# Two head pairs of a delta rule in opposite halves of the matrix array, their products by turns

## The chip, the cores and the metric

The kernel runs on one core of one Trainium2 chip. The metric is the device time of one execution in microseconds (us), taken as the median of several runs. One execution more is profiled, and everything below that is told of single instructions comes from its trace.

## The reference, cut to what matters

The program is a trunk of two layers for 256 positions and width 2048: an attention layer, a gated MLP, a layer of RWKV-7 time mixing, and a second gated MLP. The change touches the time mixing alone, 32 heads of width 64 with a matrix state each:

```python
def step(state, inp):
    r_t, w_t, k_t, v_t, kk_t, a_t = inp
    sa = jnp.einsum('bhvk,bhk->bhv', state, -kk_t)
    state = (state * w_t[:, :, None, :] + sa[..., None] * (kk_t * a_t)[:, :, None, :]
             + v_t[..., None] * k_t[:, :, None, :])
    return state, jnp.einsum('bhvk,bhk->bhv', state, r_t)

s0 = jnp.zeros((B, H, N, N), f32)
_, o = lax.scan(step, s0, (tmaj(r4), tmaj(w4), tmaj(k4), tmaj(v4), tmaj(kk), tmaj(a4)))
```

The projections around it are dense products of 2048 by 2048, whose weights are split into a high and a low part.

## The kernel before

**Staging.** The 32 heads are worked off in eight quads of four heads. A quad holds two pairs of heads, z = 0 and z = 1; a pair has 128 channels, so it fills the 128 partitions. The 256 positions are cut into four chunks c of 64, and within a chunk the recurrence is written in closed form: two triangular matrices per head and chunk, the inverse of one of them, and then a walk over the four chunks in which the state `st` is carried.

**What fills TensorE.** The generator `drive` weaves two strands. The filling strand is `quad_in` of the next quad: dense products in units of two K tiles, each unit being four matmuls (lines 154 and 155, or 157 at the end of a sum), with the DVE and ACT work for their weights (`w_hi` on ACT, line 131; `w_lo` on DVE, line 134). The other strand is `quad` of the present quad, a chain in which each step waits for the one before. Where `quad` says `yield n`, n dense units are issued before its next step, so that the evacuation of one step is done while TensorE works on dense units. All yields of a quad add up to 32, the number of units in `quad_in`. The last quad runs over units of the output projection instead, about two for each yield of 1. On TensorE, DVE and ACT the order of instructions is the order of the code; a wait in one of them holds up everything behind it on that engine.

**Steps of `quad` that the change touches**, in order of the code:

- Key norms: `pn` (line 856), then on DVE `kkt` (860), the operands `bk` (861) and `ar` (863); `yield 4`.
- Products of `bk` and `ar` (876) into `AQ`, the transposes of `bk` (888) into `tm`; `yield 4`.
- First level of the inverse by doubling: 901 on TensorE, 903, 905 and 906 on DVE; `yield 1`. Then the levels 2 to 16, each with a product 917, a `yield 1`, a product 928 and a `yield 1`. These work on 32 by 32 tiles, four of them by turns.
- The walk over the chunks c = 0 to 3. In each chunk, with e = c % 2, half e of the 128 partitions holds the chunk's rows of keys, and the other half receives: the state's part (975, not for c = 0), product A (979, contraction over 64 partitions, output in the other 64), an ACT copy to `R` (982), a dense unit, product B (994, `Z` by `R`), a DVE copy to `UV` (996), a dense unit, the state's increment (1003, not for c = 3), product C (1006, contraction over 128, output in 64 partitions), the new state on DVE (1012, 1014), an ACT copy of the chunk's result to `on2` (1021), and one or two dense units.

Each of A, B and C consists of four products, for two pairs z and two heads h. Each stands in the trace as two matmuls, so a step shows as eight. Before the change, all eight of a step use the same half of the partitions for input and the same half for output. The increment (1003) goes the other way: its two heads write to the two halves, and the code issues them by turns. It is the same for the products 876, which read their two heads from the two halves by turns.

The names of banks: `pc` is a part of the twin `pp`, two PSUM banks, one for each pair z. `pU` is one bank `sc` that holds both pairs.

Of the kernel before, what the change touches and what calls it, by code (L numbers as in the profile page):

```python
# [10 lines left out]
F32 = mybir.dt.float32  # L11
F32R = mybir.dt.float32r
AF = mybir.ActivationFunctionType
ALU = mybir.AluOpType
# [3 lines left out]
P = 128  # L18
# [35 lines left out]
class Trunk:  # L54
# [670 lines left out]


    def quad_in(self, j, sp, w, part):

        nc, a, cc, hv = self.nc, self.a, self.cc, self.hv
        tt, act = nc.vector.tensor_tensor, nc.scalar.activation  # L730
        c4 = lambda t: t.rearrange("p (c t) -> p c t", c=4)
# [17 lines left out]
        def receptance(z):  # L749

            ge = lambda t: t.rearrange("p (g e) t -> p g e t", e=2)
            rr = sp.tile([P, S], F32, name="kr", bufs=2)
            rrs.append(rr)
            self.fold(rr, prs[z])
            tt(d["ar"][:, z, :, 0::3], ge(c4(rr)), ge(d["E"][:, z])[:, :, :, 1:65], op=ALU.mult)
            if z == 0:
                nc.vector.scalar_tensor_tensor(rr, rr, self.v("rk", 2 * j), d["kp"][:, 0], op0=ALU.mult, op1=ALU.mult)
# [11 lines left out]
        for z in range(2):  # L769
            p = 2 * j + z  # L770
# [15 lines left out]
            ta = d["ta"][:, z]  # L786
# [7 lines left out]
            E, Ei = d["E"][:, z], d["Ei"][:, z]  # L794
# [3 lines left out]
            kp, g = d["kp"][:, z], flat(cs)[:, 0:S]  # L798
# [35 lines left out]
    def quad(self, j, sp, w):  # L834


        nc, a, cc, vt = self.nc, self.a, self.cc, w["vt"]
        mm, tt = nc.tensor.matmul, nc.vector.tensor_tensor
        Q = range(2)
# [7 lines left out]
        bk = sp.tile([P, 4, 256], F32, name="bk", tag="bkuv")  # L847
        kp4 = d["kp"].rearrange("p z (c e t) -> p (z c) e t", c=2, e=2)
        Ei4 = d["Ei"].rearrange("p z (c e) t -> p (z c) e t", e=2)
        for e in range(2):  # L850
            nc.gpsimd.tensor_mul(bk[:, :, 192 * e:192 * e + 64], kp4[:, :, e], Ei4[:, :, e, 1:65])
        pn = self.bank("sc")
        for z in Q:
# [6 lines left out]
        tt(k2, k2, pn, op=ALU.mult)  # L860
        tt(bk[:, :, 64:192], d["ta"].rearrange("p z (c t) -> p (z c) t", c=2),
           d["kk"].rearrange("p z (c t) -> p (z c) t", c=2), op=ALU.mult)
        tt(d["ar"].rearrange("p z g a t -> p (z g) a t")[:, :, 1:3],
           d["kk"].rearrange("p z (g e t) -> p (z g) e t", g=2, e=2),
           d["E"].rearrange("p z (g e) t -> p (z g) e t", e=2)[:, :, :, 0:64], op=ALU.mult)
        yield 4

# [18 lines left out]
        for z in Q:  # L886
            for c in range(3):
                nc.tensor.transpose(pts[z][:, c * P:(c + 1) * P], bk4[z][:, c], self.ident)
            nc.scalar.copy(flat(tm[:, z]), pts[z][:, 0:384])
# [16 lines left out]
        nc.vector.transpose(flat(Z), flat(X))  # L906
        yield 1

        vq = vt[:, :, 2 * j * P:2 * (j + 1) * P]
        UV = sp.tile([P, 2, 4, P], F32, name="UV", tag="bkuv")  # L910
        for li, b in enumerate(LEVELS):
# [9 lines left out]
            if li < 2:  # L921
                nc.scalar.copy(UV[hs[li], :, li::2], vq[hs[li]].rearrange("p c (z n) -> p z c n", z=2))
            elif li == 2:
                self.sums([d["rk"]], d["bo"][:, 1:2])
# [42 lines left out]
        for c in range(4):  # L967
            g, e = c // 2, c % 2
            hv, hu = hs[e], hs[1 - e]
            uh = lambda z, h: UV[:, z, c, 64 * h:64 * h + 64]  # L970

            pc = po[:, :, c * P:(c + 1) * P]
            if c:
                for z in Q:
                    mm(pc[:, z], ar4[z][:, c], st[:, 2 * z:2 * z + 2].rearrange("p h n -> p (h n)"),
                       start=True, stop=False)
# [13 lines left out]
            yield 1  # L990
            pU = self.bank("sc").rearrange("p (z n) -> p z n", z=2)
            for z in Q:
                for h in range(2):
                    mm(pU[hu, z, h * 64:h * 64 + 64], Z[hu, 4 * z + 2 * h + g], R[hu, z, h * 64:h * 64 + 64],
                       start=True, stop=True)
            nc.vector.tensor_scalar_mul(UV[hu, :, c], pU[hu, :, 0:P], -1.0)
            if c == 3:
                self.moments(d, s6, 0, 1)
            yield 1
            if c < 3:  # L1000
                for z in Q:
                    for h in range(2):
                        mm(pU[hs[h], z, P:P + 64], tm[:, z, c, hs[h]], uh(z, h), start=True, stop=True)
            for z in Q:
                for h in range(2):
                    mm(pc[hv, z, h * 64:h * 64 + 64], AQ[:, 4 * z + 2 * h + g, e, 64 * e:64 * e + 64], uh(z, h),
                       start=c == 0, stop=c == 0 or h == 1)
            if c < 3:
# [10 lines left out]
                else:  # L1019
                    self.moments(d, s6, 0, 0)  # L1020
            nc.scalar.copy(on2[hv, :, g], pc[hv])
            yield (2, 2, 1, 0)[c]
# [241 lines left out]
```

## Time and profile before

| | us |
|---|---|
| median of 3 runs | 2532.43 |
| lowest, highest | 2531.91, 2534.03 |
| the profiled execution, device time | 2531.73 |
| its span from the first to the last instruction | 2529.9 |
| TensorE busy in the span | 2472.4 (98%) |
| VectorE (DVE) busy | 1822.3 (72%) |
| ScalarE (ACT) busy | 1291.8 (51%) |
| GpSimd (POOL) busy | 426.0 (17%) |
| mean granted clock of TensorE | 0.989 of full speed |

The quads stand between about 1250 and 1725 us of the span. A row of a timeline gives the start, the duration, the engine, the line and the tiles; rows of the same kind that follow each other are merged, "x8" being eight of them, and the duration then runs from the first start to the last end. Matmuls overlap, since each takes longer from start to end than the distance to the next.

### The profile page before, as it was taken

How to read it: one execution, taken by the hardware profiler on the slowest of the kernel's cores; microseconds unless marked ns; L12 is line 12 of the kernel's file. 1: busy time of each engine (PE TensorE's matmuls, PEld its weight loads, DVE VectorE, ACT ScalarE, POOL GpSimd, SP SyncE). 2: the span in 40 equal slices, each digit the busy share in tenths (PEclk: the TensorE clock that was granted, in tenths of full speed). 3: DMA queues.
4: the chain of work that ended last, by engine and by line, in shares of the span. 5: the costliest groups of instructions: out<-in, count | busy, mean ns of one | idle time of the engine just before them, and what ended most of it. 6: DMA issues, size and time to landing. Idle time of an engine off the chain costs nothing.

```text
span 2529.9 us, 50155 instructions
## 1 busy us (share of the span) xinstructions
PE 2472.4 (98%) x19492; PEld 2125.1 (84%) x19492; DVE 1822.3 (72%) x3550; ACT 1291.8 (51%) x2706; POOL 426.0 (17%) x650
## 2 busy tenths in 40 slices
PE   8999999999999999989999999999999999999998
PEld 7888888888888888877877777788888888888887
DVE  7768778888888645478676676777888888884544
ACT  6468655555555444454444454445555555554443
POOL 3100112222222100000122222212222222220000
PEclk9999999999999999999999899999999999999999
DMA  7554555655555666646422223235555565556664
GB/s 264 169 181 153 165 181 187 192 190 186 192 189 189 186 189 190 186 140 184 150 91 86 80 92 100 79 119 160 175 190 190 187 191 191 187 186 191 190 187 144
DMA packets 125342, 422.36 MB, mean 167 GB/s; under 512 B 14000, under 2 KB 19504, under 8 KB 125104
## 3 DMA queue, kind: packets, MB, share of 16 engines
q1 hardware_dynamic: 124960, 418.82, 52.3%
q8 instruction: 153, 2.51, 0.4%
q14 instruction: 85, 0.70, 0.1%
q10 hardware_dynamic: 144, 0.33, 0.0%
HBM read 417.00 MB, written 2.10 MB: 166 GB/s over the span
## 4 chain that ended last, share of the span: by engine, by line
PE 90%; DVE 6%; issue 2%; ACT 1%; POOL 0%; DMA 0%; SPq 0%; DVEq 0%; ACTq 0%
PE pd L186 41%; PE pd L187 22%; PE pd L154 6%; PE pd L155 3%; PE pd L189 2%; DVE w_lo L134 1%; PE sc L630 1%; PE pp L231 1%; PE pp L232 1%; PE pp L230 1%; PE pp L928 1%; PE pp L917 1%; PE pd L231 1%; PE pd L230 1%; PE pd L232 1%
## 5 line engine op out<-in xcount | busy, mean ns | idle before, releaser
L116 DVE TENSOR_TENSOR w_lo<-w_raw,w_hi 128x512 fp32r<-128x512 f32 (+1 forms) x1384 | 1052.7, 791 | 314.0 <-ACT w_hi L114 289.0
L186 PE MATMUL pd<-xc,w_hi 128*128 128x512 f32 x3000 | 1057.4, 393 | 2.4 <-DVE u L203 1.1
L114 ACT CAST w_hi<-w_raw 128x512 fp32r<-128x512 f32 (+1 forms) x1384 | 790.7, 617 | 467.2 <-PE pd L186 286.6
L187 PE MATMUL pd<-xc,w_lo 128*128 128x256 f32 x3200 | 868.5, 282 | 1.8 <-DVE w_lo L116 1.8
L186 PEld LDWEIGHTS pd<-xc,w_hi 128*128 128x128 f32 x3000 | 563.5, 188 | 120.0 <-issue 5.2
L187 PEld LDWEIGHTS pd<-xc,w_lo 128*128 128x128 f32 x3200 | 604.4, 189 | 19.1 <-DVE w_lo L116 2.3
L186 PE MATMUL pd<-hc,w_hi 128*128 128x512 f32 x1290 | 452.8, 393 | 0.0
L187 PE MATMUL pd<-hc,w_lo 128*128 128x256 f32 x1320 | 363.6, 279 | 0.0
L186 PEld LDWEIGHTS pd<-hc,w_hi 128*128 128x128 f32 x1290 | 241.7, 187 | 56.4
L187 PEld LDWEIGHTS pd<-hc,w_lo 128*128 128x128 f32 x1320 | 247.3, 187 | 2.8
L202 ACT COPY half<-pd 128x256 f32<-128x256 f32 x232 | 86.4, 372 | 238.4 <-PE pd L189 234.8
L154 PE MATMUL pd<-mx,w_hi 128*128 128x512 f32 x416 | 164.2, 426 | 0.6 <-ACT w_hi L131 0.6
L134 DVE TENSOR_TENSOR w_lo<-w_raw,w_hi 128x256 fp32r<-128x256 f32 x352 | 146.5, 444 | 19.1 <-ACT w_hi L131 18.9
L259 POOL TENSOR_TENSOR sqacc<-sqacc,sq 128x256 f32<-128x256 f32 x70 | 61.5, 879 | 492.3 <-ACT sq L251 471.7
L131 ACT CAST w_hi<-w_raw 128x512 fp32r<-128x512 f32 x176 | 100.8, 618 | 70.7 <-PE pd L157 42.5
L155 PE MATMUL pd<-mx,w_lo 128*128 128x256 f32 x448 | 122.2, 284 | 1.2 <-DVE w_lo L134 1.2
L514 POOL TENSOR_TENSOR gt<-gt,rb 128x256 f32<-128x256 f32 x88 | 56.4, 641 | 318.2 <-DVE gt L203 315.7
L154 PE MATMUL pd<-xc,w_hi 128*128 128x512 f32 x240 | 102.5, 450 | 1.0 <-ACT w_hi L131 1.0
L526 POOL TENSOR_TENSOR up<-up,rb 128x256 f32<-128x256 f32 x88 | 65.9, 749 | 216.1 <-ACT w_hi L114 209.5
L311 ACT CAST hc<-up 128x256 fp32r<-128x256 f32 x88 | 35.9, 408 | 125.6 <-POOL up L527 125.6
L154 PEld LDWEIGHTS pd<-mx,w_hi 128*128 128x128 f32 x416 | 79.2, 191 | 18.6 <-issue 1.2
L527 POOL TENSOR_TENSOR up<-up,sg 128x256 f32<-128x256 f32 x88 | 93.6, 1064 | 6.9
(284 smaller groups left out, 3197.3 us busy)
## 6 DMA issues: line engine op xcount, KB each, us to landing
w_raw<-w_up SPq DMA_DIRECT2D x352, 512.0 KB, 4.3
w_raw<-w_dn SPq DMA_DIRECT2D x160, 512.0 KB, 3.7
w_raw<-w_kr SPq DMA_DIRECT2D x64, 512.0 KB, 3.8
w_raw<-w_eva SPq DMA_DIRECT2D x48, 512.0 KB, 4.2
w_raw<-w_out SPq DMA_DIRECT2D x32, 512.0 KB, 3.9
w_raw<-w_v SPq DMA_DIRECT2D x32, 512.0 KB, 3.9
w_raw<-w_evb SPq DMA_DIRECT2D x31, 512.0 KB, 4.5
w_raw<-w_dn SPq DMA_DIRECT2D x32, 256.0 KB, 2.7
```

The lines of the kernel that those rows point to most:

```text
L114: nc.scalar.copy(hi[h], raw[h])
L116: nc.vector.tensor_sub(lo[h], raw[h], hi[h])
L131: nc.scalar.copy(hi[:, j:e], raw[:, j:e])
L134: nc.vector.tensor_sub(lo[:, j:j + pieces], raw[:, j:j + pieces], hi[:, j:j + pieces])
L154: nc.tensor.matmul(o, h, xc[k], start=k == 0, stop=False)
L155: nc.tensor.matmul(o[:, 0:S], l, xc[k][:, 0:S], start=False, stop=False)
L186: nc.tensor.matmul(o, h, xc[k], start=k == 0, stop=False)
L187: nc.tensor.matmul(o[:, 0:S], l, xh, start=False, stop=False)
L202: self.nc.scalar.copy(t, o[:, S:2 * S])
L259: nc.gpsimd.tensor_add(self.nacc, self.nacc, sq)
L526: nc.gpsimd.tensor_mul(up, up, self.rb)
L527: nc.gpsimd.tensor_mul(up, up, sg)
```

## The change

It has three parts.

1. **The second pair in swapped halves.** For z = 1 the two chunks of a pair of chunks are written to `ar` and `bk` in reverse order (slices with a negative step, as `3 * z::3 - 6 * z`), so that in chunk c pair 0 works from half e and pair 1 from half 1 - e (`sl = [e ^ z for z in Q]`). Everything that reads these takes the index `c ^ z`. The products A, B and C are issued with h outside and z inside (`hz`), so that neighbours belong to different halves.
2. **Evacuations by pair.** An instruction that served both pairs in one half of the partitions now becomes two, one per pair: the ACT copies to `R`, to `on2` and to `UV` from `vq`, the DVE copy to `UV`, and the DVE products for `bk` and `ar`. POOL's two products for `bk` stay two, and are cut by pair where they were cut by half.
3. **Dense units.** `yield 4` after the key norms becomes `yield 3`, and `yield 1` after the first level of the inverse becomes `yield 2`. The sum stays 32.

The diff, without the lines on `UV` from `vq`, on the index of the transposes and on `on2`, which follow the same pattern:

```diff
-            tt(d["ar"][:, z, :, 0::3], ge(c4(rr)), ge(d["E"][:, z])[:, :, :, 1:65], op=ALU.mult)
+            tt(d["ar"][:, z, :, 3 * z::3 - 6 * z], ge(c4(rr)), ge(d["E"][:, z])[:, :, :, 1:65], op=ALU.mult)
...
-        for e in range(2):
-            nc.gpsimd.tensor_mul(bk[:, :, 192 * e:192 * e + 64], kp4[:, :, e], Ei4[:, :, e, 1:65])
+        for z in Q:
+            nc.gpsimd.tensor_mul(bk5[z][:, :, 3 * z::3 - 6 * z], ge(d["kp"][:, z]),
+                                 d["Ei"][:, z].rearrange("p (c e) t -> p c e t", e=2)[:, :, :, 1:65])
...
-        tt(bk[:, :, 64:192], d["ta"].rearrange("p z (c t) -> p (z c) t", c=2),
-           d["kk"].rearrange("p z (c t) -> p (z c) t", c=2), op=ALU.mult)
-        tt(d["ar"].rearrange("p z g a t -> p (z g) a t")[:, :, 1:3],
-           d["kk"].rearrange("p z (g e t) -> p (z g) e t", g=2, e=2),
-           d["E"].rearrange("p z (g e) t -> p (z g) e t", e=2)[:, :, :, 0:64], op=ALU.mult)
-        yield 4
+        mid = (slice(1, 3), slice(2, 0, -1))
+        for z in Q:
+            tt(bk5[z][:, :, mid[z]], ge(d["ta"][:, z]), ge(d["kk"][:, z]), op=ALU.mult)
+            tt(d["ar"][:, z, :, mid[z]], ge(d["kk"][:, z]),
+               d["E"][:, z].rearrange("p (g e) t -> p g e t", e=2)[:, :, :, 0:64], op=ALU.mult)
+        yield 3
...
         nc.vector.transpose(flat(Z), flat(X))
-        yield 1
+        yield 2
...
-            hv, hu = hs[e], hs[1 - e]
+            sl = [e ^ z for z in Q]
+            hv, hu = [hs[s] for s in sl], [hs[1 - s] for s in sl]
+            hz = [(h, z) for h in range(2) for z in Q]
...
+            for h, z in hz:
+                mm(pc[hu[z], z, h * 64:h * 64 + 64], AQ[hv[z], 4 * z + 2 * h + g, sl[z], 64 * (1 - sl[z]):64 * (2 - sl[z])],
+                   uh(z, h)[hv[z]], start=c == 0, stop=c == 0 or h == 1)
+            R = sp.tile([P, 2, P], F32, name="R", tag="Rg")
             for z in Q:
-                for h in range(2):
-                    mm(pc[hu, z, h * 64:h * 64 + 64], AQ[hv, 4 * z + 2 * h + g, e, 64 * (1 - e):64 * (2 - e)],
-                       uh(z, h)[hv], start=c == 0, stop=c == 0 or h == 1)
-            R = sp.tile([P, 2, P], F32, name="R", tag="Rg")
-            nc.scalar.copy(R[hu], pc[hu])
+                nc.scalar.copy(R[hu[z], z], pc[hu[z], z])
...
+            for h, z in hz:
+                mm(pU[hu[z], z, h * 64:h * 64 + 64], Z[hu[z], 4 * z + 2 * h + g], R[hu[z], z, h * 64:h * 64 + 64],
+                   start=True, stop=True)
             for z in Q:
-                for h in range(2):
-                    mm(pU[hu, z, h * 64:h * 64 + 64], Z[hu, 4 * z + 2 * h + g], R[hu, z, h * 64:h * 64 + 64],
-                       start=True, stop=True)
-            nc.vector.tensor_scalar_mul(UV[hu, :, c], pU[hu, :, 0:P], -1.0)
+                nc.vector.tensor_scalar_mul(UV[hu[z], z, c], pU[hu[z], z, 0:P], -1.0)
...
-            for z in Q:
-                for h in range(2):
-                    mm(pc[hv, z, h * 64:h * 64 + 64], AQ[:, 4 * z + 2 * h + g, e, 64 * e:64 * e + 64], uh(z, h),
-                       start=c == 0, stop=c == 0 or h == 1)
+            for h, z in hz:
+                mm(pc[hv[z], z, h * 64:h * 64 + 64], AQ[:, 4 * z + 2 * h + g, sl[z], 64 * sl[z]:64 * sl[z] + 64], uh(z, h),
+                   start=c == 0, stop=c == 0 or h == 1)
```

On TensorE the number of instructions is the same, and within a step of the walk only the order of equal shapes changes, which the diff shows. What moves there is the dense unit. Before, between the first level (901, by the constant `csr`) and the next level's first product (917, by `X`), in the second quad:

```order
L155 MATMUL pd<-mx,w_lo 128x256 x2
L157 MATMUL pd<-mx,w_hi 128x512
L901 MATMUL pp<-csr,AQ 32x16 x32
L154 MATMUL pd<-mx,w_hi 128x512
L155 MATMUL pd<-mx,w_lo 128x256
L154 MATMUL pd<-mx,w_hi 128x512
L155 MATMUL pd<-mx,w_lo 128x256
L917 MATMUL pp<-X,AQ 32x16 x32
```

The same place on TensorE in the changed program, where these two products are on lines 903 and 919:

```order
L903 MATMUL pp<-csr,AQ 32x16 x32
L154 MATMUL pd<-mx,w_hi 128x512
L155 MATMUL pd<-mx,w_lo 128x256 x2
L157 MATMUL pd<-mx,w_hi 128x512
L154 MATMUL pd<-mx,w_hi 128x512
L155 MATMUL pd<-mx,w_lo 128x256
L154 MATMUL pd<-mx,w_hi 128x512
L155 MATMUL pd<-mx,w_lo 128x256
L919 MATMUL pp<-X,AQ 32x16 x32
```

The unit that ends a dense sum now stands behind the first level; it is missing ahead of the products 876 (now 878).

On DVE before, at the key norms of the second quad (`kkt`, `bk` and `ar` are the operands of the products 876; `on`, `s` and `mv` belong to the normalization of the quad before):

```order
L755 TENSOR_TENSOR ar<-kr,E 128x2x2x64
L860 TENSOR_TENSOR kkt<-kkt,sc 128x512
L861 TENSOR_TENSOR bk<-ta,kkt 128x4x128
L863 TENSOR_TENSOR ar<-kkt,E 128x4x128
L1028 BN_STATS s_13455<-on 128x6
```

On DVE in the changed program:

```order
L756 TENSOR_TENSOR ar<-kr,E 128x2x2x64
L862 TENSOR_TENSOR kkt<-kkt,sc 128x512
L865 TENSOR_TENSOR bk<-ta,kkt 128x2x128
L866 TENSOR_TENSOR ar<-kkt,E 128x2x128
L865 TENSOR_TENSOR bk<-ta,kkt 128x2x2x64
L866 TENSOR_TENSOR ar<-kkt,E 128x2x2x64
L1033 BN_STATS s_13459<-on 128x6
```

Both operands of pair 0 now stand ahead of those of pair 1.

On ACT before, at the end of the walk in the first quad (`half` is a piece of a dense sum):

```order
L131 CAST w_hi<-w_raw 128x512 x2
L1021 COPY on<-pp 64x2x128
L982 COPY R<-pp 64x256
L1021 COPY on<-pp 64x2x128
L202 COPY half<-pd 128x256
```

On ACT in the changed program:

```order
L131 CAST w_hi<-w_raw 128x512 x2
L1026 COPY on<-pp 64x128 x2
L987 COPY R<-pp 64x128 x2
L1026 COPY on<-pp 64x128 x2
L202 COPY half<-pd 128x256
```

Each copy has become two of half the width; nothing else has moved there.

## Rows read from the trace of the kernel before

**Rows 1.** Page: busy time of TensorE; the chain that ended last, by engine

```profile
PE 2472.4 (98%) x19492; PEld 2125.1 (84%) x19492; DVE 1822.3 (72%) x3550; ACT 1291.8 (51%) x2706; POOL 426.0 (17%) x650
...
PE 90%; DVE 6%; issue 2%; ACT 1%; POOL 0%; DMA 0%; SPq 0%; DVEq 0%; ACTq 0%
```

**Rows 2.** Windows: stretch, busy time (instructions) by engine, granted clock, DMA share, GB/s

```profile
1500.00:1600.00 100.00, 94.76 (x1634) 77.88 (x1633) 70.54 (x203) 45.38 (x107) 24.38 (x39) 1.00 0.28 90
```

**Rows 3.** Groups by form, TensorE, 1260 to 1800: busy us, mean ns, idle before

```profile
L979 PE MATMUL pp<-UV,AQ 64*64 64x64 f32 x256 | 22.0, 227 | 2.9 <-ACT Z L950 2.8
L994 PE MATMUL sc<-R,Z 64*64 64x64 f32 x256 | 22.0, 227 | 0.0
L1006 PE MATMUL pp<-UV,AQ 128*64 128x64 f32 x256 | 21.0, 226 | 0.0
...
L1003 PE MATMUL sc<-UV,tm 128*64 128x64 f32 x192 | 11.1, 238 | 0.0
```

**Rows 4.** Timeline of TensorE, chunk c = 2 of the first quad

```profile
1299.84 0.68 PE L979 MATMUL pp<-UV,AQ 64*64 64x64 f32 x8
1300.45 0.50 PE L154 MATMUL pd<-xc,w_hi 128*128 128x512 f32 x1
...
1301.34 0.67 PE L994 MATMUL sc<-R,Z 64*64 64x64 f32 x8
...
1302.84 0.45 PE L1003 MATMUL sc<-UV,tm 128*64 128x64 f32 x8
1303.13 0.63 PE L1006 MATMUL pp<-UV,AQ 128*64 128x64 f32 x8
1303.69 0.44 PE L830 MATMUL sc<-ident,kr 128*128 128x128 f32 x2
```

**Rows 5.** Timeline of the same chunk: evacuations, and the next chunk's first step

```profile
1300.61 0.37 ACT L982 COPY R<-pp 64x256 f32<-64x256 f32 x1 [1.61 <-PE pp L979]
...
1302.06 0.43 DVE L996 TENSOR_SCALAR UV<-sc 64x256 f32<-64x256 f32 x1 [0.33 <-PE sc L994]
...
1303.69 0.52 DVE L1014 TENSOR_TENSOR st<-sr,fss 128x256 f32<-128x256 f32 x1
...
1304.66 0.61 PE L975 MATMUL pp<-st,ar 128*128 128x128 f32 x4
```

**Rows 6.** Groups by form, ACT and DVE, 1260 to 1800: PSUM reads of other widths

```profile
L202 ACT COPY half<-pd 128x256 f32<-128x256 f32 x31 | 11.5, 371 | 2.1 <-PE pd L189 1.6
...
L889 ACT COPY tm<-sc 128x384 f32<-128x384 f32 x8 | 3.9, 485 | 0.0
...
L1012 DVE TENSOR_TENSOR sr<-srs,sc 128x128 f32<-128x128 f32 x16 | 4.6, 288 | 4.2 <-PE sc L1003 3.9
```

**Rows 7.** Timeline from the key norms to the products 876, second quad

```profile
1309.69 0.50 PE L154 MATMUL pd<-mx,w_hi 128*128 128x512 f32 x1
...
1310.18 0.47 DVE L755 TENSOR_TENSOR ar<-kr,E 128x256 f32<-128x256 f32 x1
...
1310.57 0.68 DVE L860 TENSOR_TENSOR kkt<-kkt,sc 128x512 f32<-128x512 f32 x1
...
1311.35 0.69 DVE L861 TENSOR_TENSOR bk<-ta,kkt 128x512 f32<-128x512 f32 x1
...
1311.96 0.69 DVE L863 TENSOR_TENSOR ar<-kkt,E 128x512 f32<-128x512 f32 x1
...
1312.79 1.16 PE L876 MATMUL sc<-ar,bk 64*128 64x128 f32 x16
```

**Rows 8.** Waits of TensorE, 1260 to 1800: us in total, times, longest

```profile
PE pp L917 <- DVE X L905: 6.4, 7, 1.4
```

**Rows 9.** Timeline behind the first level, second quad

```profile
1320.87 0.72 PE L917 MATMUL pp<-X,AQ 32*32 32x16 f32 x64 [0.83 <-DVE X L905]
```

**Rows 10.** Windows of TensorE: stretch, busy time (instructions), granted clock, DMA share, GB/s

```profile
1390.00:1400.00 10.00, 10.00 (x211) 0.51 0.19 67
1400.00:1410.00 10.00, 10.00 (x52) 0.50 0.18 54
```

More of the change, by code (lines that the diff above doesn't have):

```diff
@@ L847, in quad @@
         bk = sp.tile([P, 4, 256], F32, name="bk", tag="bkuv")
-        kp4 = d["kp"].rearrange("p z (c e t) -> p (z c) e t", c=2, e=2)
-        Ei4 = d["Ei"].rearrange("p z (c e) t -> p (z c) e t", e=2)
-        for e in range(2):
-            nc.gpsimd.tensor_mul(bk[:, :, 192 * e:192 * e + 64], kp4[:, :, e], Ei4[:, :, e, 1:65])
+        ge = lambda t: t.rearrange("p (g e t) -> p g e t", g=2, e=2)
+        bk5 = [bk[:, 2 * z:2 * z + 2].rearrange("p c (a t) -> p c a t", a=4) for z in Q]
+        for z in Q:
+            nc.gpsimd.tensor_mul(bk5[z][:, :, 3 * z::3 - 6 * z], ge(d["kp"][:, z]),
+                                 d["Ei"][:, z].rearrange("p (c e) t -> p c e t", e=2)[:, :, :, 1:65])
         pn = self.bank("sc")
@@ L887, in quad @@
             for c in range(3):
-                nc.tensor.transpose(pts[z][:, c * P:(c + 1) * P], bk4[z][:, c], self.ident)
+                nc.tensor.transpose(pts[z][:, c * P:(c + 1) * P], bk4[z][:, c ^ z], self.ident)
             nc.scalar.copy(flat(tm[:, z]), pts[z][:, 0:384])
@@ L921, in quad @@
             if li < 2:
-                nc.scalar.copy(UV[hs[li], :, li::2], vq[hs[li]].rearrange("p c (z n) -> p z c n", z=2))
+                for z in Q:
+                    nc.scalar.copy(UV[hs[li ^ z], z, li::2], vq[hs[li], :, z * P:(z + 1) * P])
             elif li == 2:
@@ L974, in quad @@
                 for z in Q:
-                    mm(pc[:, z], ar4[z][:, c], st[:, 2 * z:2 * z + 2].rearrange("p h n -> p (h n)"),
+                    mm(pc[:, z], ar4[z][:, c ^ z], st[:, 2 * z:2 * z + 2].rearrange("p h n -> p (h n)"),
                        start=True, stop=False)
+            for h, z in hz:
+                mm(pc[hu[z], z, h * 64:h * 64 + 64], AQ[hv[z], 4 * z + 2 * h + g, sl[z], 64 * (1 - sl[z]):64 * (2 - sl[z])],
+                   uh(z, h)[hv[z]], start=c == 0, stop=c == 0 or h == 1)
+            R = sp.tile([P, 2, P], F32, name="R", tag="Rg")
             for z in Q:
-                for h in range(2):
-                    mm(pc[hu, z, h * 64:h * 64 + 64], AQ[hv, 4 * z + 2 * h + g, e, 64 * (1 - e):64 * (2 - e)],
-                       uh(z, h)[hv], start=c == 0, stop=c == 0 or h == 1)
-            R = sp.tile([P, 2, P], F32, name="R", tag="Rg")
-            nc.scalar.copy(R[hu], pc[hu])
+                nc.scalar.copy(R[hu[z], z], pc[hu[z], z])
             if c == 1:
@@ L1020, in quad @@
                     self.moments(d, s6, 0, 0)
-            nc.scalar.copy(on2[hv, :, g], pc[hv])
+            for z in Q:
+                nc.scalar.copy(on2[hs[e], z, g], pc[hv[z], z])
             yield (2, 2, 1, 0)[c]
```

## The prediction

> **What bounds the kernel now.** I read the page first: TensorE is busy for 98% of the span and holds 90% of the chain that ended last [rows 1]. The windows show that this holds in the time mixing too: 94.8 us of 100 on TensorE against 70.5 on DVE and 45.4 on ACT [rows 2]. So what counts is TensorE's time step by step, and an evacuation only where TensorE waits for it. The groups of the walk come next [rows 3]: A, B and C (979, 994, 1006) take 22.0, 22.0 and 21.0 us for 256 matmuls each, 82 to 86 ns apiece, while the increment (1003) takes 11.1 us for 192, which is 58 ns apiece. The shapes of 1003 and 1006 are the same, 128 rows by 64 columns with 64 moving columns; what differs is that 1003 changes the half of the output partitions at every product and 1006 doesn't. The timeline of one chunk shows the same [rows 4]: eight matmuls of A in 0.68 us, of B in 0.67, of C in 0.63, of the increment in 0.45. Last, the waits: in the quads TensorE's only large wait for DVE is for `X` ahead of 917, 6.4 us in seven times [rows 8].
>
> **Products by turns.** A: eight in 0.45 in place of 0.68, saving 0.23 us a step. B: 0.45 for 0.67, saving 0.22. C stands right behind the increment, whose eight have the next step starting 0.29 us after their own start, while C has it 0.56 after [rows 4]. Its last matmul must still drain ahead of another shape; A has 0.61 us from its start to the next shape's, and 0.45 from its first start to its last (0.68 less one duration of 0.23 [rows 3]), so leaving the shape costs 0.15. So C by turns takes between 0.29 and 0.39, and saves 0.17 to 0.27; I take 0.21. That makes 0.66 us a chunk. There are 256/8 = 32 chunks (8 quads of 4), so 21.1 us. One chunk lies in the stretch of half clock [rows 10], where everything costs about double: 0.6 more. Sum 21.7.
>
> That 64-row tiles run side by side in the same way has a row of its own: 16 matmuls of 876, on 64 rows by turns with 128 moving columns, take 1.16 us [rows 7], four of 975 on all 128 rows take 0.61 [rows 5]. With one duration (0.27) taken off, that is (1.16 - 0.27)/15 = 0.059 against (0.61 - 0.27)/3 = 0.113 each.
>
> **Two rules of the Trainium skill speak against parts of it.** First, the increment and C use all 128 rows, and the rows show turns in output halves at 0.45 against 0.63 us [rows 4]. The Trainium skill (TensorE: Matmul & The Clock Gate, "The mechanism" in Part 3) says that a weight load overlaps matmuls in flight only when the row group differs; by that C would gain nothing and the sum would be 6.7 us smaller (32 x 0.21). This trace disagrees. Second, B writes both pairs into one PSUM bank from different row halves. 917 does the like in row quarters: 64 matmuls into one bank in 0.72 us [rows 9], 11 ns each at most, where A's 64x64 tiles in one half need about 65 (0.45/7). The Trainium skill (TensorEngine Tiling, "Gotcha 1: PSUM Pressure") says that different row tiles cannot access the same bank at once; by that B would gain nothing, 7.0 us (32 x 0.22). This trace disagrees where the partitions differ.
>
> **Evacuations by pair.** One ACT copy to `R` of 64x256 takes 0.37; the PSUM copies of 128x256 and 128x384 take 371 and 485 ns [rows 6], so 128 columns cost 0.114 and a copy of 64x128 about 0.26. Two in a row end 0.26 (first) + 0.26 = 0.52 after the start at most, 0.15 later than now. `R` is done at 1300.98 and B starts at 1301.34 [rows 4, 5]: 0.36 us of room. Upper bound, if half the width costs as much as the whole: 0.74, 0.37 later, so 0.01 too late plus the semaphore. For `UV` on DVE: 128 columns take 288 ns in the nearest row [rows 6], two 0.58 against 0.43, 0.15 later; the room is from 1302.49 to 1302.84, 0.35, of which the hop from DVE to TensorE takes about 0.14 (863 ends at 1312.65, 876 waits for it and starts at 1312.79 [rows 7]). So 0.06 is left. Upper bound 0.43 later: 0.22 too late. The new state is done at 1304.21 and 975 starts at 1304.66 [rows 5]; with C 0.21 shorter ahead of it, 0.24 is left of 0.45, enough for the hop. So I cost all splits at nothing: one dense unit covers them. If the cover fails by the upper bounds, they cost 32 x (0.06 + 0.22) = 9 us. The copies to `on2` and to `UV` from `vq` add about 0.15 us each on ACT, 45% busy, and nobody on TensorE waits for them soon.
>
> **The moved dense unit.** Ahead of 876, DVE now works `kkt`, `bk`, `ar` from 1310.57 to 1312.65. A unit between equal shapes takes 0.71 us (the first after small matmuls 0.89, from 1300.45 to 1301.34 [rows 4]; 0.89 + 3 x 0.71 from 1309.69 gives 1312.71, so 876 waits 0.08 now). With three units TensorE arrives at 1312.00. The first half of 876 needs only pair 0's operands, each 128x256 (755: 0.47, next start 0.39 later [rows 7]): 1311.35 + 0.33 to 0.39 + 0.47 = 1312.15 to 1312.21, plus the hop 1312.29 to 1312.35. The wait becomes 0.3 to 0.35, so 0.25 is lost, in eight quads 2.0 us. Pair 1's operands follow some 0.7 later, while pair 0's products take 0.97. What is queued behind the wait on TensorE is the chain itself; on DVE `AQ`'s masks wait.
>
> Behind the first level the unit covers up to 0.71 of a wait of 6.4/7 = 0.9. Between the bounds: if DVE is ready as soon as now counted from 876, all 6.4 less a rest of 0.2 x 7 is won, 5.0. If DVE, with the same list of `w_lo` ahead of 903, arrives no sooner, only the time that TensorE loses at 876 comes back, and it is nothing net: 0. DVE's list is one `w_lo` shorter up to `AQ`, so I take the middle and a little: 4.5 - 2.0 = 2.5 us won net, range -2 to +5.
>
> **Sum.** 21.7 + 2.5 = 24.2. The profiled execution took 2531.73, 0.70 under the median: 2507.5 for it, and 2508 for the median.
>
> **Rivals.**
> - *One step does not pair.* The matmuls of B, whose two pairs write one bank, or those of C, whose two pairs read the same rows, stay one behind the other although they change halves. Against it stand [rows 4, 9]; for it, that no row shows exactly 64x64 tiles across both halves. Time 2508 + 7 = 2515. Chance 0.09.
> - *The split evacuations arrive late.* DVE's room is 0.06 us; `w_lo` pieces may stand between the two. 9 us back: 2517. Chance 0.08.
> - *The half-clock stretch goes.* Around 1390 to 1410 the clock is granted at 0.5 [rows 10], the lower level of 1.2 GHz; the first 10 us of it hold 211 matmuls against 52 in the second, so it begins among the small products of the doubling levels. One more dense unit ahead of them may keep it at 2.4 GHz: 20 us at half speed, 10 us won, 2498. Chance 0.08. The Trainium skill (TensorE: Matmul & The Clock Gate, Part 1) says that idleness of the matrix array lowers the clock; that would make it this way round.
> - *The change does not do what it says:* the matmuls by turns run at the old distance, as each pair waits for the other, and only the 2.5 us of the unit remain: 2530. Chance 0.04.
> - *Slower:* to move between two 64x64 tiles costs as much as to leave a shape, 0.15 us [rows 4] in place of 0.065 (0.45/7). In A and B seven times a step: 7 x 0.085 x 64 = 38 us lost, against 9 us from C and the unit: 2561. It decides from 0.085 us a step on (0.065 + 9/448). Against it: 876 and 1003 change tile all the time [rows 4, 7]. Chance 0.03.
>
> **How the numbers follow.** The forecast has 0.68, with its own range from 2503 to 2514 (the unit's net from +5 to -2 and C's 0.27 to 0.17 us a step). With the first three rivals the range is 2498 to 2517. Faster or slower counts beyond 0.2%, 5 us, about what a measurement of this kernel can tell: faster 0.93, same 0.04, slower 0.03.
>
> **What would show it.** Right: groups of A, B and C at 55 to 60 ns a matmul, eight of A in 0.45 us, no new idle time of TensorE ahead of 994 and 1003, the wait for `X` ahead of 917 below 3 us and one for `ar` ahead of 876 of about 0.3 a quad. Wrong: a group that keeps 82 ns (then its tiles don't pair), waits for `R` or `UV` of 0.1 us or more in most chunks, or a stretch of half clock at another place, which would move the time by 10 us without any of this.

## The result and the profile after

The changed kernel took 2519.11 us (median of 6 runs, 2514.17 to 2520.12) beside 2532.02 us of the kernel before: ratio 0.9939, interval 0.992 to 0.9959, so 10 to 20 us less. Forecast were 2508 us, with a range of 2498 to 2517. The direction is right. The gain is 13 us (15 by the ratio) where the sum had 24. The time lies 2 us above the range; by the ratio (0.9939 of the 2532.43 us that the forecast started from, 2517) it lies at the range's end. Two later series of the same kernel, beside the kernel before on other chips, gave less still: 0.9970 (0.9955 to 0.9985) and 0.9972 (0.9956 to 0.9987). So about half the forecast gain or less arrives.

The groups of the four steps of the walk on TensorE, 1250 to 1800 us, as in [rows 3]: shape, count, busy us, mean ns of one, idle time ahead.

```profile
L983 PE MATMUL pp<-UV,AQ 64*64 64x64 f32 x256 | 14.6, 233 | 4.2 <-ACT Z L953 4.2
L998 PE MATMUL sc<-R,Z 64*64 64x64 f32 x256 | 14.4, 232 | 0.0
L1010 PE MATMUL pp<-UV,AQ 128*64 128x64 f32 x256 | 13.9, 225 | 0.0
L1008 PE MATMUL sc<-UV,tm 128*64 128x64 f32 x192 | 10.8, 234 | 1.5 <-DVE UV L1001 0.6
```

A (now line 983), B (998) and C (1010) fell from 22.0, 22.0 and 21.0 us to 14.6, 14.4 and 13.9: 57, 56 and 54 ns a product, where 55 to 60 were named as the sign of pairing. One chunk on TensorE's timeline (start, duration), to be read beside [rows 4]:

```profile
1405.00 0.45 PE L983 MATMUL pp<-UV,AQ 64*64 64x64 f32 x8
1405.38 0.50 PE L154 MATMUL pd<-xc,w_hi 128*128 128x512 f32 x1
...
1406.27 0.45 PE L998 MATMUL sc<-R,Z 64*64 64x64 f32 x8
1406.65 0.50 PE L154 MATMUL pd<-xc,w_hi 128*128 128x512 f32 x1
...
1407.54 0.45 PE L1008 MATMUL sc<-UV,tm 128*64 128x64 f32 x8
1407.82 0.40 PE L1010 MATMUL pp<-UV,AQ 128*64 128x64 f32 x8
1408.16 0.39 PE L718 MATMUL pa<-tl,w_hi 96*128 96x256 f32 x1
```

From A's first start to the next shape's are 0.38 us (0.61 before), the same for B, and 0.34 for C (0.56): by the medians 0.23 saved in each, where the sum had 0.23, 0.22 and 0.21. So the gross gain of some 22 us is there, and the question is who took half of it back. TensorE's waits in the quads (us in total, times, longest), in place of [rows 8]:

```profile
PE pp L919 <- issue: 6.4, 5, 1.9
PE sc L878 <- DVE ar L866: 4.4, 7, 2.1
PE pp L983 <- ACT Z L953: 4.2, 6, 0.7
PE pp L931 <- issue: 3.8, 5, 1.3
```

The wait for `X` ahead of 919 (917 before) is gone, as forecast. Its line has the same 6.4 us again, under "issue": time in which TensorE waited for no other engine. The products (878) wait 4.4 us for `ar`, 2.1 of them in quad 0.

The traces of this and the later runs, summed over quads 0 to 6. The walk runs from a quad's first A to the next quad's products, so that the dense unit that moved away from there counts in it; the levels run from the start of the first looped doubling level (917, now 919) to the start of the last, unlooped one. "Half" is the time at half clock inside the levels. The last column is the sum and the number of the pauses between neighbouring small products of one group (917 and 928, now 919 and 931) of over 0.35 us, where 64 otherwise start within 0.55 us, some 9 ns apart; this one is over all eight quads.

```
trace                    walk us   levels us   half us   pauses us (number)
before                   185.8     116.2       11.3       9.3 (12)
before, second           184.8     123.1       23.9       9.6 (8)
after                    166.6     123.6       21.8      12.0 (10)
after, second            168.8     129.3       27.8      15.7 (11)
after, third             168.2     130.3       38.4      13.5 (10)
pairs alone              168.6     128.0       57.6       6.9 (5)
code shifted             167.0     118.1       10.2      12.5 (12)
```

The walk is 17 us shorter. The levels, in which the change moved nothing on TensorE, are 8 us longer on average (127.7 against 119.7). That is where most of the missing gain stands in these traces: 4 us in pauses, and 4 us at half clock (levels less pauses against the half-clock time in this table: 0.3 us for each us). The 8 us are a mean of few traces, 116 to 123 us before and 124 to 130 after, each of a run within 3 us of its kernel's median. Two near kernels of the next section, without turns and with quad 0's unit at its old place, have 120.4 and 120.2 us, in runs 11 and 6 us under their medians. So the levels' length goes with the run, and how much of the 8 belongs to the change is open.

### The profile page after: what moved, and what is told of

It is laid out like the page before. It is cut to its first block, busy times and chain, and to the rows that moved or that the text cites. A ratio compares the mean times of both kernels' runs of the same rounds, so it can differ in the third digit from the quotient of the medians.

```text
span 2517.1 us, 50314 instructions
## 1 busy us (share of the span) xinstructions
PE 2452.9 (97%) x19492; PEld 2102.1 (84%) x19492; DVE 1825.4 (73%) x3598; ACT 1305.0 (52%) x2786; POOL 430.4 (17%) x650
## 4 chain that ended last, share of the span: by engine, by line
PE 89%; DVE 5%; ACT 2%; issue 2%; POOL 1%; DMA 0%; SPq 0%; DVEq 0%; ACTq 0%; POOLq 0%
PE pd L186 41%; PE pd L187 22%; PE pd L154 5%; PE pd L155 3%; PE pd L189 2%; PE sc L630 1%; PE pp L231 1%; PE pp L232 1%; PE pp L230 1%; PE pp L931 1%; PE pp L919 1%; PE pd L231 1%; PE pd L230 1%; PE pd L232 1%; DVE w_lo L134 1%
```

## The experiments

All runs, each beside the kernel before on its chip. The clock is the mean granted clock over a kernel's runs. The last column multiplies time and clock run by run, to compare kernels at equal clock. It overcorrects: among the runs of one kernel, where there are six or more, 0.01 of clock goes with 13 to 21 us, while the product takes off 25.

```
kernel                    median us   ratio (95% interval)       clock    us x clock
before (82 runs)          2532 to 2533                            0.989   2505.5 to 2506.3
before, second (1 run)    2535.68                                 0.988   2505.3
after                     2519.11     0.9939 (0.9920 to 0.9959)   0.9892  2490.6
after, second             2526.52     0.9970 (0.9955 to 0.9985)   0.9858  2490.2
after, third              2524.32     0.9972 (0.9956 to 0.9987)   0.9868  2490.9
pairs alone               2530.31     0.9992 (0.9978 to 1.0007)   0.9833  2487.5
unit alone                2538.73     1.0024 (1.0011 to 1.0038)   0.9884  2508.4
halves, no turns          2526.58     0.9975 (0.9958 to 0.9991)   0.9857  2490.5
less on VectorE           2514.56     0.9936 (0.9918 to 0.9953)   0.9873  2483.3
pairs, filled             2535.26     0.9995 (0.9979 to 1.0012)   0.9892  2505.4
product on GpSimd         2521.20     0.9955 (0.9938 to 0.9972)   0.9885  2492.6
code shifted              2518.28     0.9952 (0.9935 to 0.9968)   0.9909  2495.8
products repeated         2562.53     1.0128 (1.0106 to 1.0151)   0.9758  2500.7
quad 0 at old place       2521.92     0.9960 (0.9944 to 0.9977)   0.9875  2490.0
```

**The pairs alone** (the changed kernel with the dense unit where it was):

```
-        yield 3
+        yield 4
...
-        yield 2
+        yield 1
```

> The swapped halves and products by turns alone, with the dense units where they were (four behind the key norms, one behind the first level). Theory: the turns carry the gain (32 chunks x 0.68 us = 21.7 us of matmul time), the unit is worth only about 1 us net, because the wait for X ahead of 919 (6.4 us before) returns as the wait ahead of 878 (3.1 us now) goes; time about 1 us above the changed kernel, 2520. Rival: the moved unit is what costs 6 us in the doubling levels (instruction supply and half clock); then this kernel is about 5 us faster than the changed one, 2514.

No measurable gain: 0.9992, and neither of the two times expected came. At equal clock the pairs are worth 19 us by the last column (2487.5 against 2506.3), 11 to 16 by the runs' own rate. So the walk gained, and 8 to 13 us of it were lost to the clock, 0.9833 against 0.9897 in that series. The wait ahead of the first level says where (the waits' view, then TensorE's timeline and windows with the granted clock in the fourth quad):

```profile
PE pp L919 <- DVE X L907: 10.8, 7, 1.6
```

```profile
1434.31 0.28 PE L155 MATMUL pd<-mx,w_lo 128*128 128x256 f32 x1
1436.22 1.05 PE L919 MATMUL pp<-X,AQ 32*32 32x16 f32 x64 [1.63 <-DVE X L907]
```

```profile
1425.00:1436.00 11.00, 9.59 (x136) 1.00 0.23 74
1436.00:1446.00 10.00, 9.78 (x273) 0.50 0.38 122
```

VectorE's list a quad is as long as before while TensorE's is 2.7 us shorter, so `X` is now waited for 10.8 us in place of 6.4, and behind this pause the clock falls to half (64 small products in 1.05 us, not 0.72).

**The unit alone** (the kernel before with three units behind the key norms and two behind the first level):

```
-        yield 4
+        yield 3
...
-        yield 1
+        yield 2
```

> The kernel before with the two yields alone (three units behind the key norms, two behind the first level). Theory: wait ahead of 917 falls from 6.4 us to below 1, wait ahead of 876 rises by 0.4 us a quad to about 4; net 1 to 3 us faster than before, within noise, 2530. Rival: the moved unit costs 6 us in the levels; 2537.

Slower by 0.24%, 6 us. Without the pairs the unit takes away most of `X`'s wait (2.1 us left of 6.4) and makes a wait of 5.5 us ahead of the products, where 0.5 stood:

```profile
PE sc L876 <- DVE s L1028: 4.3, 6, 0.7
PE pp L917 <- DVE X L905: 2.1, 1, 2.1
PE sc L876 <- DVE ar L863: 1.2, 1, 1.2
```

These waits come to under 1 us more, not 6, and the traced run took 2531.09 us, 8 under its median; where the 6 us lie is not shown. As measured, the two parts are not additive: in the three series with both, clock and time are better than with the pairs alone (in two of them the intervals overlap with it). At equal clock they nearly are: 19 us less and 2 more by the last column, and about 15 less for both. So what the unit gives beside the pairs, it gives by the clock.

**Halves without turns** (the changed kernel, but pair 0's two products of a step ahead of pair 1's):

```
-            hz = [(h, z) for h in range(2) for z in Q]
+            hz = [(h, z) for z in Q for h in range(2)]
```

> The changed kernel with the four products of a step issued pair after pair (z outside, h inside) as before the change; halves still swapped, evacuations still split. Theory: the turns are what lets the halves run side by side, a step takes 0.5 to 0.6 us again in place of 0.378, and 14 to 22 us of the gain go: 2530 to 2541. Rival: two tiles in different halves run side by side in any order; steps stay at 0.38 and the time at 2519.

```profile
L1010 PE MATMUL pp<-UV,AQ 128*64 128x64 f32 x256 | 15.3, 229 | 0.0
L983 PE MATMUL pp<-UV,AQ 64*64 64x64 f32 x256 | 14.8, 233 | 3.8 <-ACT Z L953 3.8
L998 PE MATMUL sc<-R,Z 64*64 64x64 f32 x256 | 14.8, 233 | 0.0
```

A and B pair just as well without turns, 14.8 us against 14.6 and 14.4; C, on all rows, keeps three quarters and more of its gain (15.3 against 13.9 and 21.0). At equal clock the time is that of the changed kernel (2490.5). What pairs is the swapped halves; the order by turns is worth 2 us (0.05 us a step for C, 0.01 for A and B).

**Less on VectorE** (the changed kernel without pair 0's bonus product, so that part of the bonus is left out of the output):

```
-            if z == 0:
-                nc.vector.scalar_tensor_tensor(rr, rr, self.v("rk", 2 * j), d["kp"][:, 0], op0=ALU.mult, op1=ALU.mult)
```

> The changed kernel without the DVE product of the receptance with rk and the keys of pair 0 (0.48 us, once a quad, ahead of the copy to UV of chunk 2 on DVE), so the bonus term of pair 0 is left out of the computation. Theory: the waits of 0.19 us ahead of 1008 in chunk 2 and of 0.28 us ahead of and inside 980 in chunk 3 come from the length of the list on DVE, now that TensorE comes 0.23 us a step sooner; with 0.48 less in the list both go to below 0.05 and the kernel is 2 to 3 us faster than the changed one. Rival: they come from the split copy's own length (two of 0.29) and its hop; then both waits stay as they are and the time as well.

In the changed kernel TensorE is late twice in each quad's walk. Its timeline at the end of the third chunk and the start of the fourth, third quad, with VectorE's rows from the same stretch:

```profile
1413.25 0.28 PE L155 MATMUL pd<-xc,w_lo 128*128 128x256 f32 x1
1413.66 0.45 PE L1008 MATMUL sc<-UV,tm 128*64 128x64 f32 x8
...
1415.13 0.28 PE L155 MATMUL pd<-xc,w_lo 128*128 128x256 f32 x1
1415.46 0.68 PE L980 MATMUL pp<-st,ar 128*128 128x128 f32 x4
```

```profile
1412.56 0.42 DVE L134 TENSOR_TENSOR w_lo<-w_raw,w_hi 128x256 fp32r<-128x256 f32 x1
1413.01 0.59 DVE L1001 TENSOR_SCALAR UV<-sc 64x128 f32<-64x128 f32 x2
```

The same place with the one product of 0.49 us gone (its lines stand two lower):

```profile
1410.02 0.28 PE L155 MATMUL pd<-xc,w_lo 128*128 128x256 f32 x1
1410.23 0.45 PE L1006 MATMUL sc<-UV,tm 128*64 128x64 f32 x8
...
1411.71 0.28 PE L155 MATMUL pd<-xc,w_lo 128*128 128x256 f32 x1
1411.83 0.65 PE L978 MATMUL pp<-st,ar 128*128 128x128 f32 x4
```

The distance to the increment falls from 0.41 to 0.21 us and that to the state product from 0.33 to 0.12. So VectorE's list, in which a `w_lo` stands ahead of the split evacuation, makes both; with 0.07 inside the state product they cost 0.48 us a quad, 3.8 in all. What the split's own 0.16 us (two copies in 0.59 where one took 0.43) has in it, no run separates. At equal clock this kernel is 7 us ahead of the changed one, more than the two places explain; as measured, at a lower clock, it is level with its first series.

**The pairs, with the pause filled** (the first kernel of this section, with products that nothing reads):

```
+            if li == 0:
+                for _ in range(3):
+                    mm(py[:, P:3 * P], self.ident, cc("aq", 2 * P), start=True, stop=True)
```

> The pairs alone (units where they were before), plus three products of a constant per quad, 128x256 each, into columns of PSUM that nothing reads, ahead of the first of the looped doubling levels, where TensorE waited 1.5 us a quad for VectorE's X in the run of pairs alone (10.8 us in 7 waits). They take about 1.3 us a quad, inside that wait. Theory: pairs alone lost their gain because TensorE stood idle there and its clock fell right behind it (75 us at half clock, clock 0.983); with the wait filled the half-clock stretches shrink to 45 to 55 us, the mean clock is 0.988 to 0.990 and the time 2514 to 2521 us, although nothing useful was added. Rival: the clock falls because the walk now has less work in it, or the moved units saved time by covering the wait itself; then the filled kernel stays at 2528 to 2534 us at a clock of 0.983, or is slower.

The clock came back, 0.9892 in place of 0.9833, with nothing useful added. The time didn't: the products had to wait for VectorE's `Y` of the level ahead, whose PSUM tile they share (7.8 us in 7 waits), and so stood behind the pause and not in it:

```profile
PE pp L919 <- DVE Y L905: 7.8, 7, 1.2
```

At equal clock that is 13 to 18 us. So the clock follows what TensorE is given ahead of the levels; that it can be filled for nothing isn't shown.

**The changed kernel and the kernel before, once more**

> The changed kernel as it is, once more, for a second trace and more times. If its gain over the kernel before is a gross 21.7 us less fixed losses (VectorE late in the walk 3 us, the moved unit 1 to 3 us), with the granted clock as a scatter on top, the time is 2514 to 2521 us, the chunk steps take 0.378, 0.378 and 0.334 us again, the waits ahead of the inclusions and of the third chunk's state product stand at the same places, and the half-clock stretches (48 us of them inside the eight quads in the first trace) lie at other places but again start in the doubling levels. If the first trace's places of half clock belong to the program, they come again within some us.

> The kernel before as it is, for a second trace of it. If the places and the sum of the half-clock stretches belong to the program, the second trace has 48 us of them inside the quads again, the longest of 20 us at 1390 us; if they are a scatter, they lie elsewhere in the doubling levels and their sum differs by 10 us or more.

> The changed kernel as it is, on the chip of the three others, as what they are compared with. By the two series so far: 2514 to 2530 us, 3 to 15 us under the kernel before, with a product of time and mean clock of 2489 to 2492 us against 2505 to 2507 us of the kernel before.

The second series came out at 2526.52 us, over the 2514 to 2521 expected. The steps repeat: 0.378, 0.378 and 0.334 us again, the late places too. In the second and third trace the fourth chunk's state product waits 0.36 us more for VectorE in two and five quads. In the kernel before, half clock does not repeat: its longest stretch stood at 1390 us [rows 10], and its second trace shows that time at full clock and 14 us of half clock elsewhere:

```profile
1390.00:1410.00 20.00, 19.06 (x373) 1.00 0.28 84
1453.00:1467.00 14.00, 14.00 (x122) 0.51 0.14 43
```

In the changed kernel it repeats in part: in all three traces quads 0, 1 and 5 have a stretch behind the same pause, quads 2, 4 and 6 in one or two. The pauses repeat in their places. In all three traces one stands behind the 63rd product of the same group in quad 5 (1.4, 2.0 and 1.7 us from the product ahead), and half clock follows. TensorE's timeline and windows there, first trace:

```profile
1546.40 0.70 PE L931 MATMUL pp<-Y,Z 32*32 32x16 f32 x61 [0.79 <-issue]
1547.02 0.51 PE L154 MATMUL pd<-mx,w_hi 128*128 128x512 f32 x1
1547.37 0.28 PE L155 MATMUL pd<-mx,w_lo 128*128 128x256 f32 x1
1547.48 0.40 PE L154 MATMUL pd<-mx,w_hi 128*128 128x512 f32 x1
1547.72 0.28 PE L155 MATMUL pd<-mx,w_lo 128*128 128x256 f32 x1
1547.93 0.71 PE L919 MATMUL pp<-X,AQ 32*32 32x16 f32 x63
1549.87 0.23 PE L919 MATMUL pp<-X,AQ 32*32 32x16 f32 x1 [1.23 <-issue]
```

```profile
1546.00:1550.00 4.00, 2.37 (x129) 0.93 0.13 41
1550.00:1563.00 13.00, 13.00 (x167) 0.50 0.15 49
```

From one pause to the next are 61 + 4 + 63 = 128 products, each with its weight load: 256 instructions. It is so for all of them: within a quad every pause inside a group stands a multiple of 128 products from the last. The page has the other half of it (engine rows and the instruction queue):

```profile
PE 2452.9 (97%) x19492; PEld 2102.1 (84%) x19492; DVE 1825.4 (73%) x3598; ACT 1305.0 (52%) x2786; POOL 430.4 (17%) x650
...
q8 instruction: 153, 2.51, 0.4%
```

153 packets of 16.4 KB for 38,984 instructions of TensorE: 255 in each on average, and 256 as the pauses have it, since some 300 semaphore instructions are not in the count. The trace also has the start and duration of every packet of this queue, and they settle it. All 154 such pauses of the 14 traces stand at the same place of a packet of 256, and the product behind the pause starts 1.2 to 1.6 us after the latest packet has landed; in quad 5 above it landed at 1548.49 us, and the product started at 1549.87. For the other products of these groups that distance occurs in 9 to 15%. So the pauses are waits for the next packet. The next two runs test it, by moving the pauses and by adding to them.

**The code shifted by half a packet** (32 unread products at the start, while TensorE waits for its first weights):

```
+        sh = [self.bank("sc") for _ in range(BANKS["sc"])]
+        for i in range(32):
+            nc.tensor.matmul(sh[i % len(sh)][0:16, 0:16], self.mhalf, self.mhalf, start=True, stop=True)
```

> The changed kernel with 32 products of a constant, 16 by 16, at the very start of the program, where TensorE has nothing to do until 5.4 us. They are 128 of TensorE's instructions (weight loads and products) and shift all its later ones by half of 256. In the traces so far every long pause inside a group of small products in the doubling levels stands at a multiple of 256 instructions of TensorE from the one before it, and the profile's instruction queue q8 brings 153 packets of 16.4 KB for 38,984 instructions, 255 in each. Theory: the pauses are waits for the next packet. Then they move by 64 products against the work (off 1276.5, 1327.2, 1382.1 and 1434.9 us of the first trace), still one packet apart among themselves, and the half-clock stretches, which began within 1 us of such pauses, move with them; the time stays within 5 us of the changed kernel run beside it, either way. Rival: the pauses belong to places in the work (a tile, a bank); then they stand at the same products as before.

Every pause moved by 64 products against the work. In quad 1 the changed kernel's stands behind the 47th product of a group 931; one packet later and half a packet earlier is 64 products on: the 17 left of the group, a unit of four, and 43 of the next 919. There it is (that line is 922 here):

```profile
1328.26 0.55 PE L922 MATMUL pp<-X,AQ 32*32 32x16 f32 x43
1329.10 0.37 PE L922 MATMUL pp<-X,AQ 32*32 32x16 f32 x21 [0.29 <-issue]
```

Quad 5, where all three traces of the changed kernel fell to half clock behind their pause, kept its clock:

```profile
1550.00:1563.00 13.00, 11.53 (x316) 1.00 0.20 65
```

The sum of the pauses is about the same (12.5 us), but they stand elsewhere, the mean clock is 0.9909 and the time 2518.28 us, 6 us under the changed kernel beside it, although in its trace the quads begin some 4 us later than in the others. The two intervals overlap, so the gain itself is likely rather than shown; the moved pauses are shown. Nothing of the work differs. At equal clock the last column has this kernel 5 us behind, so what it gains, it gains by the clock.

**Products repeated**:

```
-            for i in range(8):
+            for i in (0, 1, 2, 3, *range(8)):
                 for q in range(4):
                     mm(py[qs[q], i * 16:(i + 1) * 16], AT(q, q % 2)[:, i], fh(X[qs[q], i]), start=True, stop=True)
```

> The changed kernel with half of each looped doubling level's first group of products issued twice (16 more products, the same results in the same places), four times a quad. On TensorE's own time, 64 small products start in 0.72 us, so 32 more instructions of product and 32 weight loads take 0.36 us a group, 0.36 x 32 = 11.5 us in all. Rival: that is the price, 10 to 13 us above the changed kernel beside it. Theory (the levels run at the pace at which instructions arrive): the repeats are 256 more of TensorE's instructions a quad, one more packet, and packets came 3.5 to 4.2 us apart where TensorE waited for them; so 8 x 3.5 to 4.2 = 28 to 34 us, less what slack the packets ahead still have, 20 to 34 us above the changed kernel, with more pauses of over 0.35 us inside the groups than the 10 and 11 of the two traces of it.

38 us slower than the changed kernel beside it, above even the upper end of the theory. The repeats' own time was put at 11.5 us; by the trace it is 8 (96 products start within 0.81 us, 64 within 0.55). The page has 161 packets in q8, eight more, one a quad. The pauses inside groups grew from 13.5 us in 10 to 22.8 in 18, and the waits read:

```profile
PE pp L931 <- issue: 11.6, 9, 2.9
PE pp L919 <- issue: 7.9, 9, 1.5
```

By 13 to 21 us for 0.01 of clock, the lower clock (0.9758 against 0.9868) accounts for 14 to 23 of the 38 us; the other 15 to 24 (10 in the last column, which overcorrects) are the repeats' own 8 and some 9 us more of pauses. So a packet more does not cost its 3.5 to 4 us as such, as the theory had it. It costs its work, the pauses that the next packets make, and the clock behind them, and the sum of these came out above the theory. The rival, the work alone as the price, is out.

**The product on GpSimd, and quad 0** (the second also alone):

```
-                nc.vector.scalar_tensor_tensor(rr, rr, self.v("rk", 2 * j), d["kp"][:, 0], op0=ALU.mult, op1=ALU.mult)
+                act(rr, rr, AF.Copy, scale=self.v("rk", 2 * j))
+                nc.gpsimd.tensor_mul(rr, rr, d["kp"][:, 0])
...
-        yield 3
+        yield 3 if j else 4
...
-        yield 2
+        yield 2 if j else 1
```

> The changed kernel with two edits that leave no work out: pair 0's bonus product leaves VectorE (its scaling goes to ScalarE, the multiplication to GpSimd), and quad 0 alone keeps the old places of the unit (four behind the key norms, one behind the first level). Theory: VectorE's list is what is late in the walk, 0.2 us ahead of the third chunk's inclusion and 0.2 us ahead of the fourth chunk's state product in each quad, and quad 0 loses some 2.3 us by the moved unit; both go, so the time falls by 4 to 6 us, to 2512 to 2515 us, with gaps of 0.21 and 0.12 us at those two places. Rival: the product is no cause but one of many, or GpSimd and ScalarE hand it on late; then 2518 us or more, with the wait at the transposes of the sums.

> The changed kernel with one edit: quad 0 alone keeps the old places of the unit (four behind the key norms, one behind the first level). In quad 0 of the changed kernel the state products waited 2.1 us for VectorE, where the other quads wait 0.3 to 0.4. Theory: 2 us faster than the changed kernel beside it, at an equal clock; the wait ahead of the products of quad 0 goes, and a wait for X of about 1 us returns in that quad. Rival: instructions arrive no sooner, so the pause ahead of the next packet takes up what is won, and the time is the same within 1 us.

The first didn't do what was hoped: the wait for the evacuation of the third chunk grew to all eight quads (the waits' view, then VectorE's timeline in the third quad).

```profile
PE sc L1009 <- DVE UV L1002: 4.5, 8, 0.6
```

```profile
1407.18 0.42 DVE L134 TENSOR_TENSOR w_lo<-w_raw,w_hi 128x256 fp32r<-128x256 f32 x1
1407.64 0.59 DVE L1002 TENSOR_SCALAR UV<-sc 64x128 f32<-64x128 f32 x2
```

ScalarE scales ahead of its `tanh`, what VectorE does behind that comes later, and again a `w_lo` is ahead of the evacuation, whose product started at 1406.38 us. So the rival's time held (2521.20, 2518 or more), though the wait stands at the evacuation and not at the transposes: taking the product away helps, handing it on does not. Its ratio is still lower than that of the changed kernel in that series (0.9955 against 0.9970), with quad 0's edit in it and overlapping intervals. Quad 0's edit alone gave 2521.92 against 2524.32, 2.4 us, with quad 0 at 49.2 us in place of 53.6 to 54.6. The intervals of the two ratios overlap. The wait of 2.1 us that the edit was to take away stands in the first two traces of the changed kernel but is 0.5 us in the third, the one of this series, and of the quad's 4.4 to 5.4 us all but some 0.6 lie in the levels, with no half clock in them here. So the theory's 2 us fit the time but are not shown. No version ran that joins it with the shifted code.

## Why the prediction was right and wrong

- **Products by turns, 21.7 us: right in size, and wrong in its reason.** All three steps paired, to 0.01 us a step. But the term was argued from tiles that alternate at every product, and the run without turns shows that the halves alone do it, all but 2 us. Neither of the two rules weighed against it held: C and B came down as A did.
- **Split evacuations at nothing: too small.** In three chunks of four it held: from B to what follows `UV` the time fell by the step's full 0.23 us, from 1.50 to 1.27. But the room of 0.06 us was counted against a TensorE that comes at the old time. With each step 0.23 us shorter TensorE is sooner at every later wait, and VectorE's list isn't; in the third chunk that shows. Measured are 0.48 us a quad, 3.8 us, nearer to nothing than to the rival's 9.
- **The moved unit, 2.5 us won: argued wrongly, since it was costed against the kernel before.** There, alone, it loses 6 us. Its range of -2 to +5 doesn't follow from its bounds either, which are nothing to 3 us net. In quads 1 to 6 of the changed kernel it wins 0.5 us each by the steps (0.33 from C to the products, 0.20 from 903 to 919), 3 us; quads 0 and 7 lose 2.3 of them in the first two traces and 0.7 in the third. The wait for `X` went as named, but the levels did not keep what was won: 919 waits 6.4 us for its instructions where 2.9 stood before (5.4 in the second trace of before). For what would be late next, the prediction looked at engines alone; it was the instruction queue.
- **The levels at their old length: the step that failed.** The sum takes them over from the trace of before at no cost, and in the traces they came out 8 us longer: 4 in pauses, 4 at half clock. That a step or a filled wait brings TensorE sooner to its next packet of instructions is not in the sum. How much of the 8 us is scatter is open. The rival "the half-clock stretch goes" treated that stretch as part of the program; it was gone in the second trace of the same kernel. The mean clock differs with where TensorE pauses: 0.989 before, 0.983 with the pairs alone, 0.986 to 0.989 after, 0.991 with the code shifted. The prediction did name half clock at another place as what would move the time by 10 us.
- **The account.** 21.7 gross, less 3.8 in the walk, less 8 in the levels, and 1 to 2.5 for the unit, leave 11 to 12 us, before the 0.7 and 1.8 us of the fourth chunk's wait in two traces; the spans of these traces differ by 10.5 us, and the three series gave 13, 7 and 9.
- **The other rivals** (a step that doesn't pair, the change not doing what it says, a dear move between tiles) are out by the groups of 14.6, 14.4 and 13.9 us. The range was too narrow upwards: with runs of one kernel lying up to 20 us apart, most of it by their clock, no trace of a single execution allows an end 9 us above the forecast.

## What to carry to other kernels

Cost a change against the kernel that the rest of the change makes: where TensorE's steps shrink, every list on the other engines is late by that much sooner, and a wait that was harmless grows. In a stretch of hundreds of tiny products count instructions as well as time: look whether "issue" pauses lie a fixed number of instructions apart, since then a filled wait or a faster step only moves the pause. And where two kernels' mean clocks differ, compare several runs of each and set the clocks beside the times before believing a difference of 10 us.

## What the runs showed of the hardware

- TensorE's instructions came in packets of 16.4 KB, 256 each. At all 154 pauses, where 256 of them had run in 2.0 to 5.0 us, the next packet's first product started 1.2 to 1.6 us after the packet had landed, and TensorE had stood idle for up to 2.9 us. The pauses moved against the work when 128 instructions were put ahead of it.
- In the three traces of the changed kernel all 15 half-clock stretches of quads 0 to 6 began during a pause of 0.9 us or more between the starts of two products of TensorE, ahead of or among small products, or within 1.6 us of its end. Not every such pause has one behind it: that of 2.0 us at 1492.7 us of the first trace has none.
- Products on different row halves overlapped although four instructions of the one half stood together: with pair 0's ahead of pair 1's, eight products of A still took 0.46 us (0.45 by turns). On all rows, with only the output halves different, the order counted: C has 15.3 us against 13.9.
- Where GpSimd multiplied two tiles of 128x256 (0.72 to 0.74 us), VectorE's add of a constant over 128x256 beside it took 0.56 to 0.57 us, eight times in eight. In the other eight places of that kernel, and in all 16 of the changed kernel, with nothing of GpSimd beside it, it took 0.27 to 0.30.
